# Half blocks of the last two units in two transfers of 64 partitions each, and scatter steps of the last unit moved: one layer of convolution, attention and mixture of experts on one core

## The chip, the cores and the metric

One core of a Trainium2 chip runs the whole layer. The metric is the device time of one execution in microseconds (us). Three runs of the kernel before are shown, and one more execution was recorded by the profiler.

## What is computed

One layer on 512 tokens of 1024 channels in float32. The part that this case is about is the mixture of experts at its end. Each token goes to 2 of 32 experts, and each expert is a SwiGLU of inner width 512:

```
def expert_block(args):
    xb, e = args
    hid = jax.nn.silu(xb @ w_gate[e]) * (xb @ w_up[e])
    return hid @ w_down[e]
...
y = jnp.zeros((n, d), x.dtype).at[stok].add(y_sorted)
...
x = layer_norm(DEEPNORM_ALPHA * x + ffn + ple, ln2_g[i], ln2_b[i])
```

The weights of all 32 experts are read once: 32 x 6 MiB, most of the 233 MB that the kernel moves.

## The kernel before, in words

The experts are worked in 12 units. A unit of kind P has 2 experts with up to 64 tokens each (`CAP`), a unit of kind Q has 4 experts with up to 32. The list `KINDS` sets their order; the last two units, 10 and 11, are of kind P. A unit runs through these steps:

- **Gate and up** (`gate_up`, L999 to L1004): for each of 8 slices k of the channels, a piece of weights of 1 MiB (a tile of 128 partitions x 2 experts x 1024 columns) is multiplied with the gathered tokens. In a unit of kind P that is 4 products of 512 columns, each of which is 2 matmul instructions, so 8 instructions a piece.
- **SwiGLU** (`swiglu`, L1006 to L1009): one ACT and two DVE instructions; TensorE has nothing of this unit to do meanwhile. This is the unit's gap.
- **Transposes** (`turn_hidden`, L1011 to L1017), then **down** (`down`, L1019 to L1023): 4 pieces f of weights, 1 MiB each. In the last unit the down products are written out by hand (`last_down`, L1330 to L1340).
- **Scatter** (`scatter_pair`, L1208 to L1217, which calls `scatter`, L1032 to L1044): the unit's result y goes back to the tokens in 8 steps, for 4 tiles tt of tokens and 2 halves h of the channels. Each step is 2 matmuls into a bank `ps_s` and one DVE addition into the rows of x. The steps of a unit are done during the next unit: they are queued in a lane, behind them `place` (L990 to L997), which builds that next unit's own scatter matrix, and `pace` (L1226) takes some of them at fixed points of the unit.

How many steps each point takes is set by a table of weights: `WEIGHTS` for most units, `LAST` (L54) for unit 11. The points are, in order: after the pieces k = 1, 3, 5 and 7, after `swiglu` (in the gap), and after `turn_hidden`.

```
WEIGHTS = {"P": [1.5, 0, 1.5, 0] + [5, 2.5] + [0, 1, 0], "Q": [2, 2, 2, 1.5] + [3, 2] + [1, 2, 1]}
LAST = [4, 0, 4, 0, 2, 2]
```

All weights are loaded by the SP queue. `load_expert` (L255 to L273) issues two transfers for each piece, one for each expert of the pair: 512 KB, 128 rows of 4 KB. Every transfer signals one of 8 semaphores in turn (DMAHW0 to DMAHW7 below) and is issued only when the transfer 8 places earlier has landed, so 8 transfers are under way at most. A piece needs a free slot of 24. The last four pieces of unit 11 (u from 8) are loaded in another form (L267 to L273).

Between the down products of unit 10 and the first product of unit 11 stands `overflow` (L1065): each engine loads a count and takes a branch (L1067) around a loop that treats experts with more tokens than their capacity. With these inputs the loop's body doesn't run. Behind it come `split_out` (L1028 to L1030), which turns y of unit 10 into two parts, one half after the other, and then unit 11.

Of the kernel before, what the change touches and what calls it, by code (L numbers as in the profile page):

```python
# [18 lines left out]
P = 128  # L19
T = 512  # L20
NT = T // P
# [11 lines left out]
NU = len(KINDS)  # L33
# [17 lines left out]
WARM = 9  # L51
PLE = {5: 5, 6: 1, 7: 4, 8: 1, 9: 5}
WEIGHTS = {"P": [1.5, 0, 1.5, 0] + [5, 2.5] + [0, 1, 0], "Q": [2, 2, 2, 1.5] + [3, 2] + [1, 2, 1]}
LAST = [4, 0, 4, 0, 2, 2]  # L54


C_ID = 0
# [42 lines left out]
def hybrid_moe_layer_kernel(ctx: ExitStack, tc: tile.TileContext, xT, xtok, pT, w_in, w_conv, w_out, ln1, w_r,  # L100
                            b_r, w_e, w_last, w_pg, w_pp, ln2, cst, out):
    nc = tc.nc
# [5 lines left out]
    slots = Slots(upool, N_SLOTS)  # L108
# [48 lines left out]
    def serve(all_=True):  # L157
        while wants and slots.left():
            key, shape, dtype = wants.popleft()
            got[key] = slots.take(shape, dtype)  # L160
        if all_ and not wants:
            pump(0)

    def grab(key):
        if key not in got:
            serve(False)
        return got.pop(key)

    def need(key):
        while key not in loaded:  # L170
            pump(slots.left() - 1)
        return loaded.pop(key)
# [76 lines left out]
    for n in sorted(PLE):  # L249
        t = sum(len(v) for v in tasks.values())  # L250
        tasks[n] = list(range(t, t + PLE[n]))
    rows_of, base = w_e.rearrange("n u p i d -> (n u p i) d"), {}
    table = cpool.tile([P, NE], I32, name="table")

    def load_expert(n, j, u, t):  # L255

        if 2 * n < NFIX:
            nc.sync.dma_start(t, w_e[n, u])
            return
        for i in range(2):  # L260
            col = UNITS[n][0] + 2 * j + i
            if u == 0:
                base[col] = nc.values_load(table[0:1, col:col + 1], engines=[mybir.EngineType.SP], min_val=0,
                                           max_val=(NP - 1) * ROWS + 1)
            if n < NU - 1 or u < 8:
                nc.sync.dma_start(t[:, i], rows_of[bass.ds(base[col] + u * 2 * P, P, 2)])
        if n == NU - 1 and u >= 8:  # L267
            a, b = ((0, 512), (0, 512), (512, 768), (768, D))[u - 8]
            f, m = (u % 2 * 2 if u < 10 else 0), 1024 // (b - a)
            v = t.rearrange("p a d -> p (a d)").rearrange("p (f i n) -> p f i n", i=2, n=b - a)  # L270
            for i in range(2):
                src = rows_of[bass.ds(base[UNITS[n][0] + i] + (8 + f) * 2 * P, m * P, 2), a:b]
                nc.sync.dma_start(v[:, :, i], src.rearrange("(f p) d -> p f d", f=m))  # L273
# [16 lines left out]
    for k, e in first:  # L290
        a, b = k // 4, slice(k % 4, k % 4 + e - k)
# [173 lines left out]
    for ci, c in enumerate(order):  # L465
# [15 lines left out]
        if ci == 0:  # L481
            pair = [ps("mm") for _ in range(2)]
            for k in range(KD):
                a, b = k // 4, k % 4
# [7 lines left out]
        elif kind == "v":  # L492
            for tp in range(2):
                o = ps("mm")
                for s in range(2):
                    tt = 2 * tp + s
                    for k in range(KD):
                        a, b = k // 4, k % 4
# [8 lines left out]
        else:  # L507
            for m in range(2):
                o = ps("y" if ci == 1 else "mm")
                for k in range(KD):  # L510
                    a, b = k // 4, k % 4
# [20 lines left out]
    xres = [need(("x", j)) for j in range(2)]  # L532
# [492 lines left out]
    def halves(y, h):  # L1025
        return [quarter(y, 2 * h + i) for i in range(2)]
# [5 lines left out]
    def scatter(tt, h, pt, y, m, first=False):  # L1032
        o = ps("s")
        for i in range(2):
            nc.tensor.matmul(o, pt[0:m, tt * P:(tt + 1) * P], y[i][0:m], start=(i == 0), stop=(i == 1))  # L1035
        r = row(tt, h)
        if first:
            hs = slice(h * 512, (h + 1) * 512)
            nc.vector.scalar_tensor_tensor(r, x1h[tt // 2].t[:, tt % 2, hs].bitcast(F32), ALPHA, o, op0=ALU.mult,
                                           op1=ALU.add)  # L1040
            nc.vector.scalar_tensor_tensor(r, x1l[tt // 2].t[:, tt % 2, hs].bitcast(F32), ALPHA, r, op0=ALU.mult,
                                           op1=ALU.add)
        else:
            nc.vector.tensor_add(r, r, o)  # L1044
# [114 lines left out]
    def advance(lane):  # L1159
        c, gen = lanes[lane][0]  # L1160
        try:
            d = next(gen)
            lanes[lane][0] = (max(c - d, 0.01), gen)
            done[lane] += d
            return d
        except StopIteration:
            lanes[lane].popleft()
            return 0.0
# [21 lines left out]
    def chore():  # L1190

        while chores and (lack[0] is None or lack[0] in got):
            try:
                lack[0] = next(chores[0])
                return True
            except StopIteration:
                chores.popleft()
        return False
# [8 lines left out]

    def scatter_pair(n, y, *bufs):  # L1208
        pt = places.pop(n)
        for tt in range(NT):  # L1210
            for h in range(2):
                if n == 0 and h == 0 and tt % 2 == 0:
                    xres[tt // 2] = grab(("acc", tt // 2))
                scatter(tt, h, pt, halves(y, h), P, n == 0)
                if (tt, h) == (NT - 1, 1):
                    slots.give(*bufs)
                yield 0.45  # L1217

    scat = None
    for n in range(NU):  # L1220
        g, r = GROUP_OF[n]
        ne, cap = UNITS[n][1:]
        o = [ps("mm") for _ in range(2)]
        point = [0]

        def pace():  # L1226
            w = (LAST if n == NU - 1 else WEIGHTS[KINDS[n]])[point[0]:]
            if w[0]:
                fill(w[0] / sum(w))
            point[0] += 1  # L1230

        def pieces(u):
            return [need(("e", n, j, u)) for j in range(ne // 2)]

        if scat is not None:
            add(3.6, scat, 0)
        add(0.3, place_pair(n), 0)
        done[:] = [0.0, 0.0]
        ahead = n == GROUPS[g][-1] and g + 1 < NG
        if ahead:  # L1240
            claim(("xe", g + 1), [P, KD, GROUP], F32, True)
            if g % 2:
                claim(("pts", g + 1), [P, NT, 2 * GROUP], F32R, True)
        for t in tasks.get(n, []):
            add(3.5, ple_task(t))
        if n + 2 == min(tasks):
            chores.append(ple_start())
        for t in tasks.get(n + 1, []):
            if t % NT == 0:
                chores.append(ple_chunk(t // NT))  # L1250
        chore()
        for k in range(KD):
            bs = pieces(k)
            gate_up(o, k, [xe[g].t[:, k, r * P + i * cap:r * P + (i + 1) * cap] for i in range(ne)],
                    [b.t[:, i] for b in bs for i in range(2)])
            slots.give(*bs)
            if n == NU - 1 and k == 1:
                closed.clear()
                slots.q.rotate(-4)
            serve()  # L1260
            if k == 1 and ahead:
                select(g + 1)
                add(7.7 if len(GROUPS[g + 1]) > 1 else 5.3, gather_group(g + 1))
            if k > 0:
                chore()
            if n == 0 and k == 0:
                next(weights)
                next(steps)
            if n == 0 and k == 1:
                rank(mc, 0, NT, NE)  # L1270
                next(weights)
            if n == 0 and k == 4:
                late[0] = group_weights(0)
                next(late[0])
            if r == 0 and k == 6:
                for _ in late.pop(g):
                    pass
            if n == 2 and k == 6:
                count_blocks()
            if k % 2:  # L1280
                pace()
        h = sm("hw", [P, FE], bufs=1)
        swiglu(h, o, wsl[g][r], P)
        pace()
        ht = turn_hidden(h, P)
        pace()
        if n == NU - 1:
            drain()
            break
        o = [ps("y") for _ in range(2)]  # L1290
        if n == 0:
            for j in range(2):
                claim(("acc", j), [P, 2, D])
        for f in range(4):
            bs = pieces(8 + f)
            down(o, f, ht, [b.t[:, i] for b in bs for i in range(2)], cap)
            slots.give(*bs)
            if f == 3:
                claim("y", [P, 4 * T], F32R, True)
            serve()  # L1300
            chore()
            if f < 3:
                pace()
        y = grab("y")
        if n == NU - 2:
            overflow()
            serve()
        for h in range(2):
            split_out(halves(y.t, h), o[h], P)
        scat = scatter_pair(n, y.t, y)  # L1310
        while chore():
            pass
        if n == NU - 2:
            drain()
        if n == GROUPS[g][-1]:
            drain()
            slots.give(xe.pop(g))

    n, y, sq, diag = NU - 1, slots.take([P, 4 * T], F32R), slots.take([P, 512]), slots.take([P, 2, P])
    pt = places.pop(n)  # L1320
    sums, sqs = sm("sums", [P, 3, NT], bufs=1), sm("sqs", [P, 2, NT], bufs=1)
    lead, leadn, nmean, rstd, w = [sm(v, [P, NT], bufs=1) for v in ("lead", "leadn", "nmean", "rstd", "w")]
    u = sm("u", [P, 2, NT], bufs=1)
# [224 lines left out]
```

## Time and profile before

| | |
|---|---|
| runs | 763.41, 764.2, 766.37 us (median 764.2) |
| profiled execution | 763.19 us, span 761.4 us |
| PE busy | 729.0 us (96%) |
| DVE, ACT, POOL busy | 312.1, 164.0, 68.1 us |
| DMA queue of SP | 232.75 MB, 78.0% of 16 engines' span |
| expert transfers of 512 KB | 336, median 10.1 us from issue to landing |
| instruction queues | q8: 35 packets, 0.57 MB; q14: 24 packets, 0.20 MB |

Busy shares are averages over stages with different limits. What matters here is one place, from about 700 to 735 us: which engine waits there, for what, and what stands behind it. The granted clock of TensorE (PEclk, 1.00 for full speed) is given for each stretch. The two instruction queues carry the engines' own instructions.

### The profile page before, as it was taken

How to read it: one execution, taken by the hardware profiler on the slowest of the kernel's cores; microseconds unless marked ns; L12 is line 12 of the kernel's file. 1: busy time of each engine (PE TensorE's matmuls, PEld its weight loads, DVE VectorE, ACT ScalarE, POOL GpSimd, SP SyncE). 2: the span in 40 equal slices, each digit the busy share in tenths (PEclk: the TensorE clock that was granted, in tenths of full speed). 3: DMA queues.
4: the chain of work that ended last, by engine and by line, in shares of the span. 5: the costliest groups of instructions: out<-in, count | busy, mean ns of one | idle time of the engine just before them, and what ended most of it. 6: DMA issues, size and time to landing. Idle time of an engine off the chain costs nothing.

```text
span 761.4 us, 11544 instructions
## 1 busy us (share of the span) xinstructions
PE 729.0 (96%) x4328; PEld 433.7 (57%) x4330; DVE 312.1 (41%) x656; ACT 164.0 (22%) x340; POOL 68.1 (9%) x94
## 2 busy tenths in 40 slices
PE   8999999999999899999999999999999999999895
PEld 5887887787878336345623547443464445653242
DVE  4646544647588426252525113242033321223155
ACT  5445544243021101010311001200012000110024
POOL 0215335100000000000000000000000000100002
PEclk8999999999999999999999999999999999999999
DMA  8500401355509999999999999999999999999962
GB/s 303 218 1 1 166 1 34 134 227 224 211 9 367 422 413 390 386 410 408 407 410 409 397 398 354 385 410 407 401 406 387 409 409 410 408 407 410 403 204 111
DMA packets 61979, 233.52 MB, mean 307 GB/s; under 512 B 6864, under 2 KB 10592, under 8 KB 56032
## 3 DMA queue, kind: packets, MB, share of 16 engines
q1 hardware_dynamic: 61920, 232.75, 78.0%
q8 instruction: 35, 0.57, 0.3%
q14 instruction: 24, 0.20, 0.1%
HBM read 230.62 MB, written 2.10 MB: 306 GB/s over the span
## 4 chain that ended last, share of the span: by engine, by line
PE 54%; DMA 37%; DVE 5%; ACT 1%; issue 1%; SPq 1%; POOL 0%; DVEq 0%; ACTq 0%; POOLq 0%
DMA big<-in_w_e_dram 34%; PE ps_mm L1003 11%; PE ps_mm L132 6%; PE ps_mm L133 6%; PE ps_mm L134 6%; PE ps_y L1023 4%; PE ps_s L813 3%; PE ps_s L1035 3%; PE ps_y L132 1%; PE ps_z L394 1%; PE ps_y L134 1%; PE ps_y L133 1%; DMA big<-in_w_pg_dram 1%; PE ps_y L382 1%; DMA big<-in_xT_dram 1%
## 5 line engine op out<-in xcount | busy, mean ns | idle before, releaser
L1003 PE MATMUL ps_mm<-big,big 128*64 128x512 f32 (+1 forms) x1024 | 217.8, 603 | 12.5 <-DMA big<-in_w_e_dram 12.3
L1003 PEld LDWEIGHTS ps_mm<-big,big 128*64 128x64 f32 (+1 forms) x1024 | 56.6, 123 | 148.4 <-issue 86.0
L1044 DVE TENSOR_TENSOR big<-big,ps_s 128x512 f32<-128x512 f32 x80 | 52.1, 683 | 129.5 <-PE ps_s L1035 129.5
L132 PE MATMUL ps_mm<-big,big 128*128 128x512 f32 (+1 forms) x240 | 91.9, 383 | 2.2 <-ACT big L118 2.1
L133 PE MATMUL ps_mm<-big,big 128*128 128x512 f32 (+1 forms) x240 | 88.3, 368 | 0.0
L134 PE MATMUL ps_mm<-big,big 128*128 128x512 f32 (+1 forms) x240 | 88.2, 367 | 0.0
L1023 PE MATMUL ps_y<-big,ht 128*32 128x512 f32 (+1 forms) x480 | 81.3, 597 | 0.7 <-ACT ht L1016 0.7
L119 DVE TENSOR_TENSOR big<-big,big 128x512 fp32r<-128x512 f32 (+1 forms) x74 | 58.5, 823 | 27.6 <-ACT big L118 27.0
L118 ACT CAST big<-big 128x512 fp32r<-128x512 f32 (+1 forms) x74 | 50.6, 726 | 42.9 <-DVE big L433 20.1
L1035 PE MATMUL ps_s<-big,pt 128*128 128x512 f32 x176 | 57.8, 432 | 0.8 <-DVE big L1044 0.6
L132 PEld LDWEIGHTS ps_mm<-big,big 128*128 128x128 f32 x240 | 46.1, 192 | 13.3 <-ACT big L118 3.6
L134 PEld LDWEIGHTS ps_mm<-big,big 128*128 128x128 f32 x240 | 46.1, 192 | 7.9 <-DVE big L119 0.5
L133 PEld LDWEIGHTS ps_mm<-big,big 128*128 128x128 f32 x240 | 46.3, 193 | 6.8 <-DVE big L119 0.5
L807 POOL TENSOR_TENSOR big<-big,ps 128x256 f32<-128x256 f32 x16 | 11.8, 734 | 399.2 <-issue 176.2
L1035 PEld LDWEIGHTS ps_s<-big,pt 128*128 128x128 f32 x176 | 28.5, 188 | 32.5 <-issue 24.7
L375 POOL TENSOR_SCALAR big<-big,rden 128x128 f32<-128x128 f32 (+3 forms) x32 | 39.1, 1233 | 70.7 <-DVE rden L373 70.7
L813 PEld LDWEIGHTS ps_s<-big,big 128*128 128x128 f32 x320 | 41.3, 189 | 5.9 <-issue 3.3
L1023 PEld LDWEIGHTS ps_y<-big,ht 128*32 128x32 f32 (+1 forms) x480 | 21.7, 122 | 39.4 <-issue 35.8
L813 PE MATMUL ps_s<-big,big 128*128 128x256 f32 x320 | 43.8, 285 | 0.1
L132 PE MATMUL ps_s<-big,big 128*128 128x256 f32 x128 | 37.0, 289 | 0.1
L134 PE MATMUL ps_s<-big,big 128*128 128x256 f32 x128 | 36.1, 282 | 0.0
L133 PE MATMUL ps_s<-big,big 128*128 128x256 f32 x128 | 36.1, 282 | 0.0
(262 smaller groups left out, 765.7 us busy)
## 6 DMA issues: line engine op xcount, KB each, us to landing
big<-in_w_e_dram SPq DMA_DIRECT2D x336, 512.0 KB, 10.1
big<-in_w_e_dram SPq DMA_DIRECT2D x24, 1024.0 KB, 15.6
big<-in_w_in_dram SPq DMA_DIRECT2D x11, 1024.0 KB, 6.3
big<-in_w_out_dram SPq DMA_DIRECT2D x4, 1024.0 KB, 5.9
big<-in_w_pg_dram SPq DMA_DIRECT2D x4, 1024.0 KB, 9.0
big<-in_xtok_dram SPq DMA_DIRECT2D x2, 1024.0 KB, 7.0
out_dram<-big SPq DMA_DIRECT2D x8, 256.0 KB, 2.2
big<-in_xT_dram SPq DMA_DIRECT2D x3, 512.0 KB, 8.6
```

Source lines behind the costliest of these rows:

```text
L118: nc.scalar.copy(hi, raw)
L119: nc.vector.tensor_sub(lo, raw, hi.bitcast(F32))
L132: nc.tensor.matmul(o, ah, bh, start=first, stop=False)
L133: nc.tensor.matmul(o, ah, bl, start=False, stop=False)
L134: nc.tensor.matmul(o, al, bh, start=False, stop=last)
L375: nc.gpsimd.tensor_scalar(pr[h][:, 0:ks], pr[h][:, 0:ks], rden[:, h:h + 1], None, op0=ALU.mult)
L807: nc.gpsimd.tensor_tensor(r, r, s, op=ALU.add)
L813: nc.tensor.matmul(o[:, 0:n], src[tt // 2].t[:, tt % 2, k * P:(k + 1) * P], pt(tt), start=(i == 0), stop=(i == 2 * NT - 1))
L1003: nc.tensor.matmul(o[a][i * m:(i + 1) * m], x, w[:, a * FE:(a + 1) * FE], start=(k == 0), stop=(k == KD - 1))
L1023: nc.tensor.matmul(o[h][r], ht[:, f, r], w[:, h * 512:(h + 1) * 512], start=(f == 0), stop=(f == 3))
L1035: nc.tensor.matmul(o, pt[0:m, tt * P:(tt + 1) * P], y[i][0:m], start=(i == 0), stop=(i == 1))
L1044: nc.vector.tensor_add(r, r, o)
```

## The change

`load_expert` splits each 512 KB transfer of units 10 and 11 (only u below 8 in unit 11) into two of 64 partitions and 256 KB. `scatter_pair` of unit 10 does the four steps of the first half of the channels before those of the second. In unit 11, two scatter steps are issued before the first product, and the table `LAST` changes.

```
-LAST = [4, 0, 4, 0, 2, 2]
+LAST = [2, 0, 2, 0, 4, 1]
...
             if n < NU - 1 or u < 8:
-                nc.sync.dma_start(t[:, i], rows_of[bass.ds(base[col] + u * 2 * P, P, 2)])
+                m = P // (2 if n >= NU - 2 else 1)
+                for a in range(0, P, m):
+                    nc.sync.dma_start(t[a:a + m, i], rows_of[bass.ds(base[col] + (u * P + a) * 2, m, 2)])
...
     def scatter_pair(n, y, *bufs):
         pt = places.pop(n)
-        for tt in range(NT):
-            for h in range(2):
...
+        turns = [(tt, h) for tt in range(NT) for h in range(2)]
+        if n == NU - 2:
+            turns.sort(key=lambda v: v[1])
+        for tt, h in turns:
...
+        if n == NU - 1:
+            for _ in range(2):
+                advance(0)
         for k in range(KD):
             bs = pieces(k)
```

Lines of the changed kernel lie 2 higher than before in the functions named here (L1003 becomes L1005, L1035 L1037, L1014 L1016, L266 L268).

**TensorE behind the branch at the end of unit 10**, before: L1067 is the branch's end, L1003 a gate-up product of unit 11 (two rows are two pieces), L1035 a scatter step's matmuls.

```order
L1083 UNCONDITIONAL_BRANCH
L1067 UNCONDITIONAL_BRANCH
L1003 MATMUL ps_mm<-big_5569,big_5098 64x512 x4
L1003 MATMUL ps_mm<-big_5642,big_5098 64x512 x4
L1035 MATMUL ps_s<-big_5792,pt 128x512 x6
L1003 MATMUL ps_mm<-big_5655,big_5098 64x512 x4
```

The same place now:

```order
L1085 UNCONDITIONAL_BRANCH
L1069 UNCONDITIONAL_BRANCH
L1037 MATMUL ps_s<-big_5832,pt 128x512 x4
L1005 MATMUL ps_mm<-big_5593,big_5098 64x512 x4
L1005 MATMUL ps_mm<-big_5668,big_5098 64x512 x4
L1037 MATMUL ps_s<-big_5832,pt 128x512 x2
L1005 MATMUL ps_mm<-big_5683,big_5098 64x512 x4
```

Two steps (4 matmuls) stand ahead of the first product, and one step instead of three behind the second piece.

**TensorE at the gap of unit 11**, before: L1014 are the transposes, the LDWEIGHTS of `rmb` begins `place`.

```order
L1003 MATMUL ps_mm<-big_5668,big_5098 64x512 x4
L1035 MATMUL ps_s<-big_5792,pt 128x512 x6
L1003 MATMUL ps_mm<-big_5683,big_5098 64x512 x4
L1003 MATMUL ps_mm<-big_5690,big_5098 64x512 x4
L1035 MATMUL ps_s<-big_5792,pt 128x512 x2
L1014 MATMUL ps_z<-cs,hw 128x128 x4
L1035 MATMUL ps_s<-big_5792,pt 128x512 x2
```

The same place now:

```order
L1005 MATMUL ps_mm<-big_5702,big_5098 64x512 x4
L1037 MATMUL ps_s<-big_5832,pt 128x512 x4
L1005 MATMUL ps_mm<-big_5719,big_5098 64x512 x4
L1005 MATMUL ps_mm<-big_5728,big_5098 64x512 x4
L1037 MATMUL ps_s<-big_5832,pt 128x512 x6
L1016 MATMUL ps_z<-cs,hw 128x128 x4
L997 LDWEIGHTS rmb
```

The gap holds three steps instead of one, none is left behind the transposes, and the stretch before the gap holds five (two of them ahead of the first product) instead of six.

**SP's queue at the first pieces of unit 11**, before; the register instruction between two transfers is left out. In brackets stand the semaphores that the transfer waits for.

```order
L266 DMA big_5569<-in_w_e_dram 128x1024 [waits DMAHW3_49,PE_49]
L266 DMA big_5569<-in_w_e_dram 128x1024 [waits DMAHW4_49]
L266 DMA big_5642<-in_w_e_dram 128x1024 [waits DMAHW5_49,PE_49]
L266 DMA big_5642<-in_w_e_dram 128x1024 [waits DMAHW6_49]
L266 DMA big_5655<-in_w_e_dram 128x1024 [waits DMAHW7_49,DVE_49]
L266 DMA big_5655<-in_w_e_dram 128x1024 [waits DMAHW0_49]
```

The same place now:

```order
L268 DMA big_5593<-in_w_e_dram 64x1024 [waits DMAHW3_49,PE_49]
L268 DMA big_5593<-in_w_e_dram 64x1024 [waits DMAHW4_49]
L268 DMA big_5593<-in_w_e_dram 64x1024 [waits DMAHW5_49]
L268 DMA big_5593<-in_w_e_dram 64x1024 [waits DMAHW6_49]
L268 DMA big_5668<-in_w_e_dram 64x1024 [waits DMAHW7_49,PE_49]
L268 DMA big_5668<-in_w_e_dram 64x1024 [waits DMAHW0_49]
```

A piece takes four of the 8 semaphores instead of two, so 2 pieces are under way at most, where 4 were.

## Rows read from the trace of the kernel before

**Rows 1.** The chain that ended last, 640 to 762 us: start, us, what.

```profile
703.42 6.30 DMA big<-in_w_e_dram
...
709.79 5.35 PE ps_mm L1003 x16
```

**Rows 2.** TensorE's instructions in order, 680 to 735 us: start, us, [idle before <-releaser].

```profile
702.69 3.60 PE L1023 MATMUL ps_y<-big,ht 128*64 128x512 f32 x16
...
709.79 5.35 PE L1003 MATMUL ps_mm<-big,big 128*64 128x512 f32 x16 [3.50 <-DMA big<-in_w_e_dram]
```

**Rows 3.** The instructions of line 1067, the branch: count, ns min/median/max, first start.

```profile
L1067 PEldq COMPARE_BRANCH  x1: 6132/6132/6132, 703.2 to 703.2; - x1
L1067 DVEq COMPARE_BRANCH  x1: 72/72/72, 703.5 to 703.5; - x1
```

**Rows 4.** SP's transfers of line 266, 690 to 740 us, and the landing of its issues.

```profile
L266 SPq MOVE big<-in_w_e_dram x18: 29/29/29, 690.6 to 711.6; - x18
L266 SPq DMA_DIRECT2D big<-in_w_e_dram x18: 333/333/333, 690.6 to 712.3; - x18
L266 SPq FUSED_REGOPS  x17: 43/46/51, 691.0 to 711.5; - x17
...
DMA to landing us min/median/max: 10.1/10.2/10.2
```

**Rows 5.** DMA queue q8 in 706.8 to 706.9 us: packets, MB, share of the engines.

```profile
q8 instruction: 1, 0.02, 68.3%
```

**Rows 6.** SP's own waits, 712 to 740 us (total, times, longest), then the queues in 730.4 to 730.6.

```profile
SPq L1067 <- SPq L1067: 8.0, 4, 3.9
...
q14 instruction: 1, 0.01, 12.8%
```

**Rows 7.** The page's DMA issues: stores at the kernel's end, KB, us to landing.

```profile
out_dram<-big SPq DMA_DIRECT2D x8, 256.0 KB, 2.2
```

**Rows 8.** The packets of two stretches: 252 to 270 us (transfers of 1 MB), 640 to 680 us (512 KB).

```profile
DMA packets 1047, 7.62 MB, mean 423 GB/s; under 512 B 117, under 2 KB 117, under 8 KB 117
...
DMA packets 4483, 16.35 MB, mean 409 GB/s; under 512 B 499, under 2 KB 499, under 8 KB 4480
```

**Rows 9.** Busy time by stretch: PE, PEld, DVE, ACT, POOL, then PEclk, DMA share, GB/s.

```profile
709.00:709.50 0.50, 0.00 (x0) 0.00 (x0) 0.00 (x0) 0.00 (x0) 0.00 (x0) 1.00 1.07 426
...
710.00:710.50 0.50, 0.50 (x2) 0.07 (x2) 0.00 (x0) 0.00 (x0) 0.00 (x0) 0.50 1.01 401
...
713.50:714.00 0.50, 0.50 (x4) 0.17 (x2) 0.00 (x0) 0.00 (x0) 0.00 (x0) 1.00 1.01 385
```

**Rows 10.** Two other idle times of TensorE, and the clock in the stretches behind them.

```profile
9.38 0.50 PE L132 MATMUL ps_mm<-big,big 128*128 128x512 f32 x1 [2.07 <-ACT big L118]
...
10.50:11.00 0.50, 0.50 (x2) 0.40 (x2) 0.00 (x0) 0.50 (x1) 0.00 (x0) 0.50 1.06 430
...
265.99 0.66 PE L1014 MATMUL ps_z<-cs,hw 128*128 128x128 f32 x4 [1.42 <-DVE hw L1009]
...
264.00:270.00 6.00, 3.90 (x22) 1.39 (x20) 1.43 (x2) 0.94 (x2) 0.00 (x0) 1.00 1.02 425
```

**Rows 11.** TensorE's and DVE's instructions around scatter steps, from 682 us on.

```profile
682.87 1.19 PE L1035 MATMUL ps_s<-big,pt 128*128 128x512 f32 x4
...
691.00 0.73 PE L1035 MATMUL ps_s<-big,pt 128*128 128x512 f32 x2
...
706.13 1.52 DVE L1030 TENSOR_TENSOR big<-ps_y,big 128x512 fp32r<-128x512 f32 x2 [2.48 <-ACT big L1029]
...
723.66 1.65 PE L1035 MATMUL ps_s<-big,pt 128*128 128x512 f32 x6
725.24 3.65 PE L1003 MATMUL ps_mm<-big,big 128*64 128x512 f32 x16
728.82 0.73 PE L1035 MATMUL ps_s<-big,pt 128*128 128x512 f32 x2
730.33 0.66 PE L1014 MATMUL ps_z<-cs,hw 128*128 128x128 f32 x4 [0.77 <-DVE hw L1009]
```

More of the change, by code (lines that the diff above doesn't have):

```diff
@@ L1209, in scatter_pair @@
         pt = places.pop(n)
-        for tt in range(NT):
-            for h in range(2):
[L1212 to L1217, printed above, removed]
+        turns = [(tt, h) for tt in range(NT) for h in range(2)]
+        if n == NU - 2:
+            turns.sort(key=lambda v: v[1])
+        for tt, h in turns:
+            if n == 0 and h == 0 and tt % 2 == 0:
+                xres[tt // 2] = grab(("acc", tt // 2))
+            scatter(tt, h, pt, halves(y, h), P, n == 0)
+            if (tt, h) == turns[-1]:
+                slots.give(*bufs)
+            yield 0.45
     scat = None
```

## The prediction, as it was made before the result

> **What bounds the kernel now.** I read the chain of waits first. Up to 709.7 us it is weight transfers; from 709.79 it is TensorE: unit 11's products, the gap, the down products and the tail [rows 1]. So the place to look at is the seam between units 10 and 11. TensorE's instructions in order show it: unit 10's last down products end at 702.69 + 3.60 = 706.29, and unit 11's first product starts at 709.79 [rows 2]. These 3.50 us of idle time are what the change can act on.
>
> Two readings offer themselves. The row names a transfer as the releaser. But SP's rows say otherwise: 18 transfers were issued from 690.6 to 712.3, one every 21.7 / 17 = 1.28 us, and each landed 10.2 us later [rows 4]. The first two are unit 10's last piece, the other 16 are unit 11's pieces 0 to 7. Piece 0's second transfer is the fourth of the 18: issued at 690.6 + 3 x 1.28 = 694.4, landed at 704.6, long before 709.79. What TensorE really waited for is the branch: on its sequencer the compare-and-branch took 6132 ns from 703.2 on, so to 709.35, while DVE's took 72 ns [rows 3]. In that time one packet of 0.02 MB began on an instruction queue, q8, at about 706.85; it took 68.3% of 16 engines for 0.1 us, so 1.1 us of one engine [rows 5]. I read this as the fetch of the code behind the skipped loop. It waited 706.85 - 703.2 = 3.65 us before it was served, while 8 transfers of 512 KB were in flight.
>
> The stall has a second price. The granted clock is 1.00 in the idle time, 0.50 behind it, and 1.00 again by 713.5 [rows 9]. The 16 matmuls of pieces 0 and 1 took 5.35 us [rows 1], where 16 at full clock take 3.65 [rows 11]: 1.7 us. An idle time of 2.07 us was followed by the low clock too, one of 1.42 us was not [rows 10].
>
> **The change, part by part.** 40 transfers more are issued: 24 for unit 10, 16 for unit 11. SP needs 333 + 29 + 46 ns, some 0.41 us, for each [rows 4]; a transfer of 256 KB lasts 0.64 us at the present rate, so SP still keeps up. Behind SP's waits on its 8 semaphores stand only later weights. A transfer is issued about 5 us before it lands instead of 10, which asks for a free slot later than now. Cost: nothing.
>
> *Rate of the halves.* No row shows a load of 64 partitions. Nearest are the 1 MB transfers at 423 GB/s against 409 for 512 KB [rows 8], so halving once cost at most 2.564 - 2.479 = 0.085 us a MiB; two transfers more a MiB cost up to 0.17. Over unit 10's 12 pieces that is 0 to 2.0 us, by the last piece of unit 11's eight 0 to 3.4. Is there room? Unit 10's last piece landed at 691.8 + 10.2 = 702.0 and was begun at about 704.4 [rows 2, 4]: 2.4 us. Piece 7 of unit 11 landed at 712.3 + 10.2 = 722.5 and was begun at about 727.0, the second half of the 16 products from 725.24 on [rows 4, 11]: 4.4 us. Both ends are hidden, so I cost this at nothing; if the cover of 4.4 us is used up, any further lateness is paid in full. The same cover limits every gain: TensorE cannot begin piece 7 before 722.5, so 4.4 us is the most that can be won ahead of the gap.
>
> *The fetch.* Only half as many bytes now lie in front of it: 8 transfers of 256 KB. Ends: nothing saved, if the 3.65 us do not depend on them; up to about 2.65, if the queue's whole part goes. For that part I take off a fixed 1.0 us, an estimate within the 2.2 us that a 256 KB store needs on a queue that is otherwise short [rows 7], 0.64 us of them data. I take half of 2.65, 1.3 us, since the bytes are halved. The idle time becomes 3.5 - 1.3 = 2.2 us, still above the 2.07 after which the clock fell, so the 1.7 us of low clock stay.
>
> [...]
>
> *The scatter steps.* Ahead of the gap, six matmuls twice (1.65 us each) become groups of 4, 2 and 4 (1.19, 0.73, 1.19) [rows 11]: 3.30 to 3.11, 0.2 us less. The two early steps need only half 0 of y, and DVE splits both halves from 706.13 to 707.65 [rows 11], before the branch ends; nobody waits. In the gap six matmuls stand where two did: 728.82 + 1.65 = 730.47, while the transposes begin at 730.33 when DVE is done [rows 11], so at most 0.14 us is given back. TensorE was idle there for 0.77 us, which is what hides the other steps; DVE's additions come after SwiGLU's in its queue and delay nothing on the path. Behind the transposes a step goes, but ACT's copy sets the pace there. Net 0.1 us gained.
>
> **The sum.** 1.3 + 0.1 = 1.4 us off the profiled execution's 763.19 (a span of 761.4, and 1.8 around it) is 761.8. The median of the runs is 1.0 above the profiled one, so the forecast is 764.2 - 1.4 = 762.8. About 0.5% (3.8 us) is what a measurement of this kernel can tell from no change; this is under it.
>
> **The rivals.**
>
> *The stall goes, and the low clock with it.* If the fetch gains 2.1 us or more, the idle time is 1.4 us or less, as in the row without a fall. Then 2.1 + 1.7 + 0.1 = 3.9 us go, 760.3; the cover caps it at 4.4, 759.8. [...] Against: it needs more than half of the wait, and halving the bytes gives half.
>
> *The fetch does not care (the change does not do this).* SP took the same branch later and waited 3.9 us, with its queue's packet at 730.4, when the transfers were already running out [rows 6]. That is the same wait with less in front of it. Then only 0.1 us is won: 764.1.
>
> *The halves move slowly: slower than before.* Each transfer now fills 64 partitions only. If these are reached over half of the paths, the 20 pieces take twice their 20 x 2.55 = 51 us, piece 7 lands 51 us later and TensorE waits 51 - 4.4 = 46.6 us: 811. It decides from a loss of rate of 4.4 / 51, 9%; at 16% the price is 3.8 us, 768.0. For it: not one load of the trace has this shape. Against: 8 transfers of both halves are in flight at once, and the 512 KB transfers lost little against 1 MB ones. [...]
>
> **How the numbers follow.** Forecast (fetch shortened by 0.3 to 2 us, clock still falls): 0.40, 762.8 with 762.0 to 763.9 of its own. Stall and low clock gone: 0.26, 760.3. Fetch unmoved: 0.17, 764.1. Halves slow: 0.17, from 768 to 811. Faster by over 0.5% is the second case and a little of the first's edge, 0.27; slower is the last, with 0.01 taken off for a loss under 16%, 0.16; within 0.5% is the rest, 0.57. The range runs from 759.0 (the cap of 4.4 us, less 0.8, by which the lowest run lay under the median) to 768.0; it leaves out most of the slow case, some 0.15.
>
> **What would show it.** Right: TensorE's compare-and-branch at about 4.8 us instead of 6.13; its idle time before unit 11 at about 2.2; unit 10's and 11's transfers landing some 5 us after issue, the queue still at about 400 GB/s; no idle time in the gap. The stall case shows a branch under 4 us and PEclk 1.00 behind it. Wrong: GB/s under 370 between 670 and 725 us, with TensorE waiting for transfers inside units 10 or 11; or a branch of 6 us as before.

## The result, and the profile after

The changed kernel takes 793.17 us (median of 4 runs, 792.38 to 793.41), the kernel before 763.96 beside it: a ratio of 1.0377, interval 1.0354 to 1.0399. It is slower by 29.2 us. The forecast of 762.8 was wrong, and so was the end of the range, 768.0. What came is the rival of the halves that move slowly.

The profiled execution took 793.19 us with a span of 791.4. First the page: the rate in 40 slices (19.8 us each), and the landing times by size of transfer.

```profile
GB/s 307 194 1 41 120 1 54 213 160 338 34 174 404 419 393 332 410 407 407 409 408 396 393 374 377 408 409 408 407 399 410 409 408 374 263 245 247 254 249 145
...
big<-in_w_e_dram SPq DMA_DIRECT2D x296, 512.0 KB, 10.1
...
big<-in_w_e_dram SPq DMA_DIRECT2D x80, 256.0 KB, 8.4
```

The rate falls with the first halves and stays down to the last one. A transfer of half the size needed 8.4 us instead of the 5 that I had expected. Busy time by stretch (PE, PEld, DVE, ACT, POOL, then PEclk, DMA share, GB/s) sets the edges, and shows the clock:

```profile
660.00:668.00 8.00, 7.95 (x60) 5.90 (x59) 2.37 (x5) 1.25 (x3) 0.74 (x1) 1.00 1.03 409
668.00:690.00 22.00, 21.02 (x148) 10.16 (x144) 4.86 (x8) 2.60 (x7) 0.00 (x0) 1.00 1.02 262
690.00:730.00 40.00, 28.35 (x96) 8.87 (x96) 7.87 (x15) 2.36 (x4) 0.00 (x0) 0.98 1.02 247
730.00:756.00 26.00, 21.76 (x67) 7.00 (x68) 3.34 (x5) 0.00 (x0) 0.00 (x0) 0.90 1.03 254
...
728.00:732.00 4.00, 0.29 (x1) 0.33 (x2) 0.00 (x0) 0.00 (x0) 0.00 (x0) 0.55 1.04 250
```

The DMA share reads 1.03 at 409 GB/s and 1.02 at 247. The engines look just as busy; each packet only takes longer: 16 engines that are busy throughout and move 4 KB a packet (in 690 to 730 us 2406 packets of 2 to 8 KB hold nearly all of the 9.89 MB) need 16 x 4096 B / 247 GB/s = 265 ns for it, 160 at 409 (worked out from these rows). Whoever reads the share alone sees no change here.

What TensorE waited for in 660 to 770 us (total, times, longest), and then the branch on its sequencer (count, ns, start):

```profile
PE ps_mm L1005 <- DMA big<-in_w_e_dram: 9.0, 11, 1.2
PE ps_s L1037 <- PEq L1069: 5.9, 1, 5.9
PE ps_y L1025 <- DMA big<-in_w_e_dram: 2.9, 3, 1.1
```

```profile
L1069 PEldq COMPARE_BRANCH  x1: 6687/6687/6687, 724.6 to 724.6; - x1
```

These waits are short because a piece trickles in and TensorE starts and stops with it. They don't add up to the loss: TensorE's idle time grew by 16.6 us over the whole span, and its busy time grew as well, from 729.0 to 742.4 us. The chain of waits shows the whole of it: from 690.85 on, one transfer after another of 7 to 9 us each, where TensorE's work had been (start, us, what):

```profile
690.85 7.12 DMA big<-in_w_e_dram
...
749.20 8.46 DMA big<-in_w_e_dram
```

TensorE's instructions in order, around the seam and at unit 11's last piece:

```profile
723.94 1.90 PE L1025 MATMUL ps_y<-big,ht 128*64 128x512 f32 x6 [1.13 <-DMA big<-in_w_e_dram]
731.71 2.05 PE L1037 MATMUL ps_s<-big,pt 128*128 128x512 f32 x4 [5.86 <-PEq L1069]
...
757.79 1.90 PE L1005 MATMUL ps_mm<-big,big 128*64 128x512 f32 x6 [1.20 <-DMA big<-in_w_e_dram]
759.63 1.65 PE L1037 MATMUL ps_s<-big,pt 128*128 128x512 f32 x6
761.12 0.64 PE L1016 MATMUL ps_z<-cs,hw 128*128 128x128 f32 x4
```

The products of piece 7 on its second expert begin at 757.79. Before, they began at about 727.0 [rows 11]: 30.8 us later, and the span is 30.0 us longer. So all of the loss lies ahead of the gap. The bytes give most of it: 80 transfers of 256 KB are 20.97 MB, 51.3 us at 409 GB/s [rows 8] and 82.9 at the 253 of these stretches (their mean by time), 31.6 more. The cover of 4.4 us that the prediction found between the landing and the use of piece 7 is to be taken off, which leaves 27.2; the other 3.6 us this sum does not explain.

The fetch did not shorten: 6.69 us on TensorE's sequencer for 6.13 [rows 3], 5.86 us idle for 3.50 [rows 2], and the clock fell as before [rows 9]. The gap behaves as forecast: six scatter matmuls, then the transposes with no idle time.

### The profile page after: what moved, and what is told of

The parts are those of the page before. It is cut to its first block, busy times and chain, and to the rows that moved or that the text cites. A ratio compares the mean times of both kernels' runs of the same rounds, so it can differ in the third digit from the quotient of the medians.

```text
span 791.4 us, 11706 instructions
## 1 busy us (share of the span) xinstructions
PE 742.4 (94%) x4330; PEld 436.3 (55%) x4330; DVE 312.1 (39%) x656; ACT 164.0 (21%) x340; POOL 68.2 (9%) x94
## 4 chain that ended last, share of the span: by engine, by line
PE 47%; DMA 44%; DVE 5%; issue 1%; SPq 1%; ACT 1%; POOL 1%; DVEq 0%; ACTq 0%; POOLq 0%
DMA big<-in_w_e_dram 40%; PE ps_mm L1005 9%; PE ps_mm L132 5%; PE ps_mm L133 5%; PE ps_mm L134 5%; PE ps_y L1025 4%; PE ps_s L815 3%; PE ps_s L1037 2%; DMA big<-in_w_pg_dram 1%; PE ps_y L134 1%; PE ps_z L396 1%; PE ps_y L132 1%; PE ps_y L133 1%; DMA cs<-in_cst_dram 1%; PE ps_y L384 1%
## 5 line engine op out<-in xcount | busy, mean ns | idle before, releaser
L1005 PE MATMUL ps_mm<-big,big 128*64 128x512 f32 (+1 forms) x1024 | 227.4, 604 | 19.3 <-DMA big<-in_w_e_dram 18.9
L1005 PEld LDWEIGHTS ps_mm<-big,big 128*64 128x64 f32 (+1 forms) x1024 | 59.8, 123 | 161.5 <-issue 95.8
L132 PE MATMUL ps_mm<-big,big 128*128 128x512 f32 (+1 forms) x240 | 90.0, 375 | 3.2 <-ACT big L118 3.2
L1025 PE MATMUL ps_y<-big,ht 128*32 128x512 f32 (+1 forms) x480 | 86.3, 605 | 3.7 <-DMA big<-in_w_e_dram 2.9
L133 PE MATMUL ps_mm<-big,big 128*128 128x512 f32 (+1 forms) x240 | 87.1, 363 | 0.2 <-DVE big L119 0.2
L134 PE MATMUL ps_mm<-big,big 128*128 128x512 f32 (+1 forms) x240 | 86.9, 362 | 0.1
L1037 PE MATMUL ps_s<-big,pt 128*128 128x512 f32 x176 | 58.7, 438 | 6.6 <-PEq L1069 5.9
L132 PEld LDWEIGHTS ps_mm<-big,big 128*128 128x128 f32 x240 | 45.4, 189 | 14.0 <-ACT big L118 4.6
L1037 PEld LDWEIGHTS ps_s<-big,pt 128*128 128x128 f32 x176 | 29.0, 191 | 39.4 <-issue 31.5
L134 PEld LDWEIGHTS ps_mm<-big,big 128*128 128x128 f32 x240 | 45.3, 189 | 7.8 <-DVE big L119 0.6
L133 PEld LDWEIGHTS ps_mm<-big,big 128*128 128x128 f32 x240 | 45.3, 189 | 6.8 <-DVE big L119 0.8
```

The costliest lines, as they stand in the source:

```text
L132: nc.tensor.matmul(o, ah, bh, start=first, stop=False)
L133: nc.tensor.matmul(o, ah, bl, start=False, stop=False)
L134: nc.tensor.matmul(o, al, bh, start=False, stop=last)
L1005: nc.tensor.matmul(o[a][i * m:(i + 1) * m], x, w[:, a * FE:(a + 1) * FE], start=(k == 0), stop=(k == KD - 1))
L1025: nc.tensor.matmul(o[h][r], ht[:, f, r], w[:, h * 512:(h + 1) * 512], start=(f == 0), stop=(f == 3))
```

## The experiments

Theory A says that the halves cost the 30 us: A1 because a transfer fills 64 neighbouring partitions, A2 because there are twice as many transfers, of half the size. Theory B says the moved scatter steps cost it. All diffs are against the kernel before, unless said otherwise.

**The halves alone, then the moved steps alone.** The first takes only the change's edit of the transfers, the second only its edit of the scatter steps.

```diff
-                nc.sync.dma_start(t[:, i], rows_of[bass.ds(base[col] + u * 2 * P, P, 2)])
+                m = P // (2 if n >= NU - 2 else 1)
+                for a in range(0, P, m):
+                    nc.sync.dma_start(t[a:a + m, i], rows_of[bass.ds(base[col] + (u * P + a) * 2, m, 2)])
```

> The kernel before with the split into two transfers of 64 partitions alone; scatter steps and their table as before. Theory A (the split is the whole loss): 792 to 796 us, the queue at about 250 GB/s from 670 us on, transfers landing some 8.4 us after issue. Rival B (the moved scatter steps cost a good part, by what they collide with): 764 to 785 us.

```diff
-LAST = [4, 0, 4, 0, 2, 2]
+LAST = [2, 0, 2, 0, 4, 1]
...
+        if n == NU - 2:
+            turns.sort(key=lambda v: v[1])
...
+        if n == NU - 1:
+            for _ in range(2):
+                advance(0)
```

> The change without the split: whole transfers of 128 partitions, scatter steps and table moved. Theory A: 763.8 us, 0.1 to 0.3 us under the kernel before, the queue at 409 GB/s, the branch of TensorE at 6.1 us as before. Rival B: 770 us or more.

The halves alone: 793.13 us (785.22 to 793.72), ratio 1.0399, interval 1.0371 to 1.0427. The whole loss. The profiled execution was the one of 785.22, and its rate was higher too:

```profile
690.00:730.00 40.00, 30.09 (x102) 10.35 (x101) 7.88 (x15) 2.35 (x4) 0.00 (x0) 0.94 1.03 280
```

The moved steps alone: 763.74 us (12 runs), ratio 1.0002, interval 0.9986 to 1.0017. They are worth nothing that can be told. Theory B is out.

**Same number and size, other partitions.** Both have the change's scatter steps, and 80 transfers of 256 KB with rows of 2 or 4 KB. The first puts every other partition into a transfer, the second all 128, with half of the columns.

```diff
+                    for a in range(2):
+                        nc.sync.dma_start(t[a::2, i], rows_of[bass.ds(base[col] + (u * P + a) * 2, P // 2, 4)])
```

> The change, but the two transfers of a half block take the even and the odd partitions (64 each, rows of 4 KB, 256 KB) instead of the lower and the upper 64. Number, size and rows of the transfers are those of the change; only which partitions one transfer fills differs. Theory A1 (the rate falls because one transfer fills one half of the partitions): the queue stays at 380 to 409 GB/s and the time is 760 to 765 us; the branch tells what the smaller transfers do to the fetch: 4.8 us if half the bytes ahead halve the wait, 6.1 if they do not matter. Rival A2 (size, number or signalling of the transfers is what costs): about 250 GB/s and 790 us or more, as in the change.

```diff
+                    for a in range(0, D, 512):
+                        nc.sync.dma_start(t[:, i, a:a + 512], rows_of[bass.ds(base[col] + u * 2 * P, P, 2), a:a + 512])
```

> The change, but a half block is split by columns: two transfers of 128 partitions with rows of 2 KB, 256 KB each. Theory A1: 360 to 409 GB/s (rows of 2 KB may cost something) and 760 to 768 us. Rival A2: about 250 GB/s, 790 us or more. The branch of TensorE again 4.8 or 6.1 us.

Every other partition: 766.83 us, ratio 1.0050 (1.0033 to 1.0068). Columns: 764.56, ratio 1.0024 (1.0005 to 1.0042). The rate, of the first and then of the second:

```profile
675.00:695.00 20.00, 20.00 (x128) 7.63 (x122) 4.60 (x10) 1.86 (x5) 0.00 (x0) 1.00 0.97 345
```

```profile
675.00:695.00 20.00, 20.00 (x126) 7.64 (x120) 4.64 (x10) 1.95 (x6) 0.00 (x0) 1.00 1.04 373
```

So 256 KB transfers cost a part of the 409 (345 and 373 are left), but most of the fall to 247 is due to which partitions a transfer fills. At 345 to 373 the cover hides the larger part: 3.7 and 1.5 us are left of 30.

**Neighbours of the same side, and the last unit alone.** In the first, the lower halves of both experts go first, then the upper halves. In the second, only unit 11 has halves.

```diff
+            for a in range(0, P, P // 2):
+                for i in range(2):
...
+                    nc.sync.dma_start(t[a:a + P // 2, i], rows_of[bass.ds(base[col] + (u * P + a) * 2, P // 2, 2)])
```

> The kernel before, with the transfers of the last two units cut into halves of 64 partitions as in the change, but in another order: the lower halves of both experts first, then the upper halves of both, so that neighbours on the queue go to the same side two by two. Theory A1 (one transfer fills one side only, and a neighbour on the other side makes up for a part of that): the rate of the stretch falls below the 247 to 283 GB/s of the changed kernel, towards half of the whole transfers' 409, that is to 205 to 240; 80 transfers of 256 KB are 20.97 MB, 51.3 us at 409 and 102.3 at 205, and less the cover of some 3 us the time is 795 to 812. Theory A1b (each side is slow by itself and the neighbours don't matter): 247 to 283 GB/s and 785 to 794 us, as the change. Theory A2 (it is the number or the size of the transfers): the same, 785 to 794.

```diff
+                m = P // (2 if n == NU - 1 else 1)
+                for a in range(0, P, m):
+                    nc.sync.dma_start(t[a:a + m, i], rows_of[bass.ds(base[col] + (u * P + a) * 2, m, 2)])
```

> The kernel before, with the halves of 64 partitions in the last unit alone: 32 transfers of 256 KB, 8.39 MB, which take 20.5 us at 409 GB/s and 29.6 to 34.0 at 283 to 247. Theory A1: the rate falls in those 30 us alone and the loss is 9 to 13.5 us less the cover of 4.4 us ahead of the last whole pieces, 768 to 773 us; unit 10 runs as before. If the loss came from how the two units follow each other, or from the state of the queue, it is not in proportion: 764 or 785 and above. The branch ahead of the last unit still costs 5.5 to 6.7 us, since its wait lies where the halves are in flight.

Paired sides: 794.95 us, ratio 1.0412 (1.0379 to 1.0446), and 253 GB/s. This other order changes nothing that can be told; that neighbours on the two sides make up for each other fell. Last unit alone: 775.3 us (773.37 to 777.1), ratio 1.0137 (1.0105 to 1.0169). The rate of the first, then of the second, where it keeps to the place of the halves:

```profile
690.00:720.00 30.00, 24.92 (x84) 7.79 (x84) 6.49 (x13) 1.18 (x2) 0.00 (x0) 1.00 1.03 253
```

```profile
680.00:700.00 20.00, 20.00 (x106) 7.41 (x105) 5.03 (x11) 2.45 (x6) 0.00 (x0) 1.00 1.03 409
704.00:740.00 36.00, 29.27 (x106) 10.53 (x102) 5.90 (x9) 1.17 (x2) 0.00 (x0) 0.95 1.01 253
```

8.39 MB at 253 are 33.2 us, 12.7 more than at 409; less the cover of 4.4 that is 8.3, and 11.5 were measured, above the 768 to 773 us expected. The loss follows the bytes in halves, but some 3 us of it the sum does not explain. In the profiled execution, the slowest of the four, a part of the lateness is older than the halves: unit 10's last down products, whose weights came in whole transfers, began at 706.52, 3.8 us later than before [rows 2]. The branch took 4.69 us, less than the 5.5 to 6.7 expected.

**Large halves, and large transfers of every other partition.** The first two units load 24 transfers of 1 MB at 423 GB/s [rows 8]. Here these alone are cut: into halves of 512 KB, as large as the whole transfers elsewhere; into 512 KB of every other partition; into quarters of 32 neighbours.

```diff
-            nc.sync.dma_start(t, w_e[n, u])
+            for a in range(0, P, P // 2):
+                nc.sync.dma_start(t[a:a + P // 2], w_e[n, u, a:a + P // 2])
```

> The kernel before, in which not the last two units but the first two (24 transfers of 1 MB, whole partitions of 8 KB) are cut into halves of 64 partitions, 512 KB each: as large as the whole transfers of the later units, which run at 409 GB/s. Theory A1 (the side of the partitions): the stretch that ran at 423 GB/s falls to 245 to 285, though no transfer is smaller than 512 KB; the 25.2 MB take 88 to 103 us for 59.5, and what of that is not hidden there is lost: 775 to 805 us. Theory A2 (size or number): 400 to 423 GB/s in that stretch and 762 to 767 us.

```diff
+            for a in range(2):
+                nc.sync.dma_start(t[a::2], w_e[n, u, a::2])
```

> As the kernel that halves the first two units' 24 transfers of 1 MB (221 to 233 GB/s, 794 us), but with every other partition instead of 64 neighbours: the same 512 KB, the same rows of 8 KB, the same number of transfers. Theory A1 (the side that is filled): 390 to 423 GB/s in the stretch of these units, 762 to 767 us, and the 350 GB/s of every other partition in the last two units is the price of 256 KB transfers of 4 KB rows. Theory A2 (64 partitions in a transfer are too few, wherever they lie): 220 to 285 and 785 to 800 us.

```diff
+            for a in range(0, P, P // 4):
+                nc.sync.dma_start(t[a:a + P // 4], w_e[n, u, a:a + P // 4])
```

> The first two units' 24 transfers of 1 MB cut into quarters of 32 neighbouring partitions, 256 KB each. Theory S (what limits is the side, and two quarters in a row go to the same one): 205 to 235 GB/s as with the halves of 64 there, 790 to 800 us. Theory P (the rate goes with the number of partitions that a transfer fills): 100 to 135 GB/s; the 25.2 MB take 187 to 252 us for the 59.5 of whole transfers and the 113 of halves, 860 to 930 us.

Halves: 794.0 us, ratio 1.0393 (1.0361 to 1.0425). Quarters: 793.38, ratio 1.0410 (1.0380 to 1.0439). Every other partition: 759.58 us, ratio 0.9949 (0.9929 to 0.9969), faster than before; what it gained is not in its transfers, as will be seen at the branch. The rates, in the order halves, every other, quarters:

```profile
240.00:270.00 30.00, 26.30 (x167) 12.76 (x167) 13.86 (x57) 5.32 (x10) 0.29 (x1) 0.95 1.02 223
```

```profile
250.00:270.00 20.00, 17.26 (x96) 5.92 (x94) 6.17 (x23) 2.88 (x5) 0.29 (x1) 0.94 1.02 423
```

```profile
240.00:270.00 30.00, 26.29 (x162) 12.59 (x162) 13.30 (x53) 4.80 (x10) 0.29 (x1) 0.94 1.02 222
```

This is the cleanest pair of the study: the same bytes, rows, sizes and number of transfers, and 223 GB/s against 423. A2 is out as the main cause. Quarters move at the rate of halves, so it does not go by the number of partitions either. One thing goes along in all of these runs: a transfer that fills neighbouring partitions also reads neighbouring rows of the weights, and no run separates the two.

**Both sides at once.** The upper halves of the last two units are issued by ScalarE, on its own queue.

```diff
+                    for a, q in ((0, nc.sync), (P // 2, nc.scalar)):
+                        q.dma_start(t[a:a + P // 2, i], rows_of[bass.ds(base[col] + (u * P + a) * 2, P // 2, 2)])
```

> The kernel before with the halves of 64 partitions in the last two units, the lower halves issued by SP as in the change and the upper halves by ScalarE, on a queue of its own, so that a lower and an upper half can be under way at once. Theory S (each side takes only a part of the rate, and one queue works its transfers off in order, so that it writes to one side at a time): the rate of the stretch comes back to 380 to 409 GB/s and the time to 762 to 768 us, unless the waits of ScalarE's transfers hold up its other work. Theory H (a transfer of 64 neighbouring partitions is slow by itself, whatever else is under way): 245 to 285 GB/s and 785 to 795 us.

822.32 us, ratio 1.0780 (1.0754 to 1.0806). The queues (packets, MB, share) in 700 to 702 us, TensorE's longest wait, and the rate:

```profile
q1 hardware_dynamic: 78, 0.25, 51.1%
q10 hardware_dynamic: 75, 0.25, 50.0%
```

```profile
PE ps_s L1040 <- ACT big L1034: 40.6, 1, 40.6
```

```profile
700.00:750.00 50.00, 17.54 (x62) 6.28 (x62) 4.68 (x11) 2.72 (x7) 0.00 (x0) 0.64 1.03 257
```

Lower and upper halves were under way together, in equal shares, and the rate was still 257. So theory S fell: it is not that one queue writes to one side at a time. The rate is the one that H gave; the time is not. It is worse because ScalarE's copies stood behind its transfers in its instruction order (ScalarE did no work for 32.1 us ahead of one copy), and TensorE behind the copies (40.6 us at one).

**What the branch is worth.** The call of the loop for experts over their capacity is left out, and with it the loop, which these inputs do not enter.

```diff
-            overflow()
```

> The kernel before without the branch to the loop for experts over their capacity (the loop is left out; it is not entered here). What the wait for the code costs: 6.13 us of wait, of which 3.50 us was idle time of TensorE, and the 16 products behind it took 5.35 us at the lower clock where such groups take 3.65 at the full one. Theory B (the wait is on the path, and transfers have the room to be late): 758.5 to 760.5 us, 3.5 to 5.2 below before. Theory C (the transfers set the end; what the branch costs is won back, since the last pieces wait for the queue): 762.5 to 765, no change that can be told.

759.59 us, ratio 0.9936 (0.9912 to 0.9960): 4.2 us less. Theory B of this run holds. Unit 11's products follow unit 10's without a pause, and take 3.60 us, as at the full clock (3.65 [rows 11]):

```profile
704.32 3.60 PE L1023 MATMUL ps_y<-big,ht 128*64 128x512 f32 x16
707.76 3.60 PE L1003 MATMUL ps_mm<-big,big 128*64 128x512 f32 x16
```

**What the branch's wait hangs on.** It was 6.13 us before, and 6.03, 5.49, 6.09, 6.15, 5.87 and 6.35 in the moved steps, every other partition, columns, halves alone, paired sides and two queues. The columns are the plainest of these: half the bytes in front of the packet, no wait more in TensorE's code, and no gain.

```profile
L1071 PEldq COMPARE_BRANCH  x1: 6092/6092/6092, 704.2 to 704.2; - x1
```

But it was 3.79, 3.69 and 2.03 in the three kernels that changed only the first two units, hundreds of us earlier. What these changed near the branch is the number of TensorE's instructions ahead of it: most products on a piece that comes in two transfers need one more wait, 19 in all with two transfers a piece and 43 with four. So I gave the kernel before more instructions at the very start, in the products of `WARM`, whose result nothing reads, and changed no transfer.

```diff
-    for _ in range(WARM):
-        nc.tensor.matmul(warm, zerob, onesb[:, 0:1].to_broadcast([P, 512]), start=True, stop=True)
+    for _ in range(31):
+        nc.tensor.matmul(warm[:, 0:148], zerob, onesb[:, 0:1].to_broadcast([P, 148]), start=True, stop=True)
```

This is the edit for 44 more instructions (22 products and their weight loads). The others have 19 products of 242 columns (20 more), 41 of 112 (64 more) and 21 of 219 (24 more).

> The kernel before, whose 9 products of 512 columns that warm TensorE at the start are 19 of 242 columns instead: 20 more instructions of TensorE long ahead of the branch, nearly the same columns, no transfer changed. The wait at the branch was 6.0 to 6.1 us where TensorE had as many instructions ahead of it as before, 3.7 to 3.8 with 19 more and 2.0 with 43 more, each time some 2.5 us past the landing of a packet of code. Theory L (the packet is asked for at a fixed place in TensorE's code, and how far the branch lies behind that place sets how much of its way is left): 3.5 to 4.0 us of wait, under 1.5 us of idle, 759 to 762 us. Theory T (those kernels gained by their transfers in the first two units): 6.0 us of wait and 763 to 766 us.

> As the kernel with 20 more instructions, with 31 products of 148 columns: 44 more instructions. Theory L: 1.5 to 2.5 us of wait at the branch, next to no idle time of TensorE, no lower clock behind it, less up to 1 us that the smaller products take at the start: 758.5 to 761.5 us, where the kernel without the branch took 759.6. Theory T: 6.0 us and 763 to 766.

> As the kernel with 20 more instructions, with 41 products of 112 columns: 64 more instructions. Theory L: the packet has landed over 2.5 us ahead of the branch, which then waits only for what else it needs: no longer than with 44 more, 0.1 to 2.5 us, and 759 to 762 us, since TensorE's queue of products covers so much; the smaller products at the start may cost up to 2 us. Theory T: 6.0 us and 763 to 767.

> The kernel before with 21 products of 219 columns at the start instead of 9 of 512: 24 more instructions of TensorE, as many as the halves of 64 partitions in the last two units give it (23). Theory L (a fixed place in TensorE's code): a wait at the branch of 3.0 to 3.8 us, between those with 20 and 44 more. Theory L2 (the address alone: beyond some 20 the packet falls back to where it was): 5.5 to 6.7 us, as in the kernels with halves in the last two units.

With 20 more: 760.44 us, ratio 0.9947 (0.9927 to 0.9967). With 44: **758.2 us**, ratio 0.9932 (0.9909 to 0.9955). With 64: 759.93, ratio 0.9949 (0.9926 to 0.9972). With 24, one run: 759.94, too few to compare. The branch, in the order 20, 24, 44, 64:

```profile
L1067 PEldq COMPARE_BRANCH  x1: 3571/3571/3571, 705.9 to 705.9; - x1
```

```profile
L1067 PEldq COMPARE_BRANCH  x1: 3165/3165/3165, 703.9 to 703.9; - x1
```

```profile
L1067 PEldq COMPARE_BRANCH  x1: 2085/2085/2085, 702.5 to 702.5; - x1
```

```profile
L1067 PEldq COMPARE_BRANCH  x1: 1465/1465/1465, 703.6 to 703.6; - x1
```

Theory L holds for these four. The packet on q8 began 3.6 us after the branch before [rows 3, 5], then 1.1, 0.7, and with 44 and 64 more 0.5 and 1.0 us ahead of it: for the one with 44, this row of 701.9 to 702.0 us.

```profile
q8 instruction: 1, 0.02, 75.7%
```

In each of these the branch ended 2.5 to 2.6 us after the packet began (began, not landed, as the expectation had it). With 44 more, TensorE was idle for 0.46 us and the 16 products then took 3.65 us, as at the full clock:

```profile
706.06 3.65 PE L1003 MATMUL ps_mm<-big,big 128*64 128x512 f32 x16 [0.46 <-PEq L1067]
```

The kernels with 20, 44 and 64 more all beat the kernel before and the changed one; which of the three is best can't be told, since their runs overlap (757.8 to 762.4, 756.6 to 761.4, 758.1 to 761.5 us).

**The same in the changed kernel.** To see whether the place still decides with halves under way, the change got the 31 products as well.

> The changed kernel with 31 products of 148 columns at the start: 44 more instructions than the change, 67 more than before. Theory L: the wait at the branch, 6.69 us in the changed kernel, falls to 1.4 to 2.5 us, though the transfers there still run at 245 to 285 GB/s; the time falls by less than the 4 to 5 us, since the transfers set the end there: 783 to 792 us. Theory S (with halves under way the packet comes late whatever the place): 5.5 to 6.7 us and 785 to 794.

One run: 786.31 us, and the branch all but gone:

```profile
L1069 PEldq COMPARE_BRANCH  x1: 450/450/450, 719.8 to 719.8; - x1
```

```profile
700.00:720.00 20.00, 17.82 (x70) 6.48 (x69) 6.32 (x13) 1.18 (x2) 0.00 (x0) 1.00 1.02 286
```

The wait shrinks here too, below the 1.4 to 2.5 us expected. Its time is below the changed kernel's 793, but its rate was higher as well (286 for 247), as in the one execution of the halves alone that took 785.22. What the pad gained here can't be told apart from that.

## Why the prediction was wrong, step by step

**"Rate of the halves … Both ends are hidden, so I cost this at nothing": this step failed.** It said itself that no row shows a load of 64 partitions, and then took its bounds from two sizes of transfers that all fill 128. Those rows bound the price of size. The edit changed the shape too, and for that the trace of before had no row. A bound from below nothing to twice the time was the honest one. It stood in the text, as the rival's 811, and should have been an end of this term and not only a case with a chance of 0.17.

What the runs showed in its place: 247 to 254 GB/s for 409 in the changed kernel, 31.6 us more for the 20.97 MB and 29.2 us more in time.

The size part was too small as well: at 345 to 373 GB/s, 20.97 MB take 4.9 to 9.5 us more than at 409; I had 0 to 3.4 by unit 11's eighth piece. The cover of 4.4 us swallowed a good part of it, as the times of 764.6 and 766.8 show. The shape took the rest.

**The rival had the event, not its reason.** It said the 64 partitions "are reached over half of the paths", which would give half of the rate. Measured were 223 GB/s for 512 KB halves, close to half of 423, and 247 to 286 for 256 KB halves, more than half of 409. Its point of decision was about right: the time grows with the bytes beyond the cover, and at a loss of 38% it grew by 29 us. Its price at 16% took a loss of rate for an equal gain of time: 51 us become 51 / 0.84 = 60.7, so 9.7 us more, 5.3 beyond the cover, and not 3.8. Every other partition, which lost 16%, was 3.7 us slower. Its reason in the simple form, that only one side works at a time, does not stand: with both sides under way in equal shares the rate was 257. How many paths serve a transfer no run shows. What "against" named, "8 transfers of both halves are in flight at once", is true and did not keep the rate from 247 GB/s.

**"The fetch": wrong in its reason and its number.** I took the 3.65 us between the branch and the packet for time in the queue and gave half the bytes half of it, −1.3 us. The branch's wait was 0.56 us longer instead, and with columns, the same bytes in front of it as in the change, it stayed at 6.09. The pads show what moves it, though the halves don't fit in yet (see Open): the number of TensorE's instructions ahead of the branch. In the kernel before, the packet began 3.65 us behind the branch's start, with 20 and 24 more instructions 1.1 and 0.7 us behind it, with 44 and 64 more 0.5 and 1.0 us ahead of it, so there it was not the branch that asked for it. The branch ended 2.5 to 2.6 us after the packet began, each time. Theory L fits this; where in the code the packet is asked for, no row shows. The packet's row [rows 5] fitted my reading and I took it as a proof. One run would have fitted it too: 4.69 us with halves in the last unit alone, near the 4.8 forecast; the other six kernels with 256 KB transfers there, at 5.5 to 6.7, do not. "The fetch does not care" named the right outcome for this term.

**Low clock: right** for the changed kernel, where the clock fell in 5.86 us of idle time, to 0.61 in 728 to 730 us and 0.50 in 730 to 732. That any idle time above 2.07 us brings it is not so: with the moved steps alone it stayed at 1.00, behind 3.39 us. **Scatter steps: right**; 0.1 us was forecast and the interval holds it. **Cover: about right in size**: by it the columns should cost 0.5 us and the last unit 8.3, and 1.5 and 11.5 were measured. **The stall's worth: right**; the rival with stall and low clock gone stood at 760.3, and 759.6 came without the branch. Only this change was not what removes it.

**Open.** Why transfers to 32 or 64 neighbours move at 222 and 223 GB/s for 423, and at 257 for 409 though others fill the other side at the same time, was not tried further. Nor is it settled why the halves in the last two units, which also give TensorE 23 more waits ahead of the branch, left its wait at 5.5 to 6.7 us, where 24 instructions at the start made it 3.17, nor why it was 4.69 us with halves in the last unit alone, which adds none ahead of it. And executions of the same halves differ: 785 to 794 us, with 247 to 280 GB/s.

## What to carry to other kernels

Split a load so that each transfer still spreads over the whole range of partitions: by columns (373 GB/s here for 409), or by every other partition (345 for 409 at 256 KB, 423 for 423 at 512 KB); 64 neighbours cost 30 to 47% of the rate here (247 to 286 for 409, 223 for 423), and the busy share of the DMA engines does not show it (1.02 for 1.03). A bound for a term is only as good as the shape of the rows it is from: when an edit changes size and shape, each needs its own. A branch that waits, as this one did, may be eased by moving it in the instruction stream, here from 6.13 us to 2.09 by 22 more products at the start; vary the number of instructions ahead of it before blaming the transfers.

## What the runs showed of the hardware that I had not expected

- 24 transfers of 1 MB in halves of neighbours: 223 GB/s; in quarters: 222; of every other partition: 423. Two queues with one side each: 257.
- TensorE's wait at a branch went from 6.13 to 3.57, 3.17, 2.09 and 1.47 us with 20, 24, 44 and 64 more instructions 700 us earlier.
- The clock did not fall behind every long idle time. With the moved steps alone it stayed, behind 3.39 us; it fell behind 3.50 us [rows 9] and 2.07 [rows 10]:

```profile
712.87 1.16 PE L1035 MATMUL ps_s<-big,pt 128*128 128x512 f32 x4 [3.39 <-PEq L1067]
```

```profile
712.00:716.00 4.00, 3.13 (x14) 1.45 (x16) 1.28 (x2) 0.00 (x0) 0.00 (x0) 1.00 1.04 412
```
